# A two-block network: half-row heads, and half of an output product set between the turns of an attention

## Chip, cores and metric

One core of one Trainium2 chip runs the whole program in one launch. The metric is device time in microseconds (us), the median of several runs. In the profile PE is TensorE (PEld its weight loads), DVE is VectorE, ACT is ScalarE, POOL is GpSimd, SP is SyncE, whose queue issues most DMAs.

## What is computed

256 tokens of width 1024 pass two blocks in fp32. The first block has a mixer (spatial gating beside a neighbourhood attention with 8 heads of 64), a convolution mixer and two MLPs. The second block, cut to what the change touches:

```python
def hybrid_mixer(h, w_in, w_out, rel_bias):
    proj = h @ w_in                      # mq, mk, mv, dq, dk, dv, iq, ik, iw
    ...
    y_moba = moba_attention(mq, mk, mv, rel_bias[:8])      # 8 heads of 64
    y_dsa = dsa_attention(dq, dk, dv, iq, rms(ik), iw * 0.5, rel_bias[8:])
    return concatenate([y_moba, y_dsa]) @ w_out            # 1024 -> 1024

def dsa_attention(q, k, v, q_idx, k_idx, w_idx, tab):
    rel = relu(einsum('bqhd,bsd->bqhs', q_idx, k_idx))     # 4 index heads of 64
    score = einsum('bqh,bqhs->bqs', w_idx, rel)            # causal
    ...                                  # the 64 best keys of each query stay
    s = q @ k * scale + bias             # 8 heads of 64, on the keys that stay
    return softmax(s) @ v
```

After it come the gated sum `x + g1 * y`, a norm, and the peer feed-forward (queries by `w_q`, products with `subkeys`, then the large tables `uT` and others).

## The kernel before

**Products.** Weights arrive as fp32 tiles of 128 x 1024 through SP's queue (L146). ACT casts each to its high part (L176, fp32r), DVE or POOL makes the low part (L177). `mm` (L182 to L185) multiplies in three matmuls, hi by hi, hi by lo, lo by hi. The work is recorded for the Tile framework, which fixes at build time the order in which each engine takes its instructions. Each engine takes its own in that order.

**Attention.** A head has 64 rows of the 128 partitions; two heads lie in one tile `kT[:, f, :]`. The queries are copied into `qz`, a tile of 8 heads by 128 rows that was zeroed by POOL (`memset`, L712 and L1047) and of which each head fills its own 64 rows (`scaled_queries`, L628 to L633, 8 ACT instructions). A head's scores (L776 in the first mixer, L1128 in the second) are matmuls over all 128 rows, the other 64 being zeros. The index heads do the same with `iq` (memset L1074, copies L1076, transposes L1089, products L1100). `probs` (L612 to L626) adds the bias and takes the row's extreme on DVE (L618), the exponential on ACT (L620), the reciprocal and the scaling on DVE (L623, L625). Then PE turns the rows (L1142), ACT copies them (L1143), and for each pair of heads PE multiplies with the values (L1148), 64 columns of the array for each of the two. DVE copies the result (L1151), ACT casts its high part (L198), DVE makes its low part (L199), both into `yT`. `pipelined` (L635) runs `scores` some heads ahead of `values` (3 in moba, 2 in dsa), and before each turn takes one step of the generator `aside`.

**The second mixer** (`mixer2`, L1053). The moba projections come first. In the turns of the moba attention stand the index heads and the projections of dsa. DVE then finds the kept keys in eight rounds (L1166, L1168) and writes `kept` (L1171). In the dsa attention POOL adds `kept` to a head's bias, one instruction for each head and row tile, 16 in all (L1132). The output product with `w_out_2` runs in four parts of 256 rows: parts 0 and 1 (moba's half of `yT`) are 48 matmuls of 128x512 (`rows_step`, recorded ahead of the dsa attention), parts 2 and 3 (dsa's half) another 48 in `rows_end` (L474). `add_gated` (L447) multiplies the sums with the gate (L454) and adds them to x (L455), tile by tile of 128 tokens. The norm's rows are turned by L398, and the products with `w_q` begin (L191 to L194). The DMA of `subkeys` (L1288) opens the peer stage; it writes into a buffer that `yT` held.

Of the kernel before, what the change touches and what calls it, by code (L numbers as in the profile page):

```python
# [15 lines left out]
OP = mybir.AluOpType  # L16
# [3 lines left out]
P = 128  # L20
D = 1024
KC = D // P
T = 256
EPS = 1e-6
NEG = -1e30
# [49 lines left out]
class Net:  # L75
# [552 lines left out]
    def scaled_queries(self, qz, pq):  # L628

        for f in range(4):  # L630
            for j in range(2):
                s = slice(64 * j, 64 * j + 64)
                self.nc.scalar.mul(qz[s, 2 * f + j, :], pq[f // 2][s, f % 2, :], 0.125)  # L633
# [75 lines left out]
    def mixer0_rest(self, h, hc, qs, pgs):  # L709
        nc, a = self.nc, self.a  # L710
        qz = self.big([P, 8, T])
        nc.gpsimd.memset(qz, 0.0)  # L712
        self.scaled_queries(qz, qs)
# [51 lines left out]
        bts, pTs = {}, {}  # L765

        def scores(hd):
            f, j = hd // 2, hd % 2
            if j == 0:
                bt = bts[f] = self.work([P, 5, T], "bias", 2)  # L770
                nc.gpsimd.memset(bt[:, 4, :], 0.0)
                nc.sync.dma_start(bt[:, 0:4, :], a["bias0"][f])
            parts = []
            for t in range(2):
                s = self.ps()
                nc.tensor.matmul(s, qz[:, hd, t * P : (t + 1) * P], kT[:, f, :], start=True, stop=True)  # L776
# [255 lines left out]
    def projections(self, b0, h, by_tile=False):  # L1032
# [12 lines left out]
        qz = self.big([P, 8, T])  # L1045
        with self.behind(self.last_pow):
            nc.gpsimd.memset(qz, 0.0)  # L1047
        for pq in self.feature_product(b0, h):
            yield
        self.scaled_queries(qz, pq)  # L1050
        yield kT, qz, v


    def mixer2(self, h, mods):
# [5 lines left out]
        def index_heads():  # L1060

            w = sum((self.weights(a["w_idx"][:, 4 * q : 4 * q + 4, :], [P, 4, 324]) for q in range(2)), [])
            iqT = self.m4([P, 4, T])
# [3 lines left out]
            for t in range(2):  # L1067
# [4 lines left out]
                iq = self.m2([P, 4, P])  # L1072
                with self.behind(self.last_pow):
                    nc.gpsimd.memset(iq, 0.0)  # L1074
                for i in range(4):
                    nc.vector.tensor_copy(iq[:, i, 64 * (i % 2) : 64 * (i % 2) + 64], pi[:, 64 * i : 64 * i + 64])  # L1076
# [9 lines left out]
            for t, (iq, ik) in enumerate(rows):  # L1086
                pt = self.ps([P, 4, P])
                for i in range(4):
# [6 lines left out]
            for t in range(2):  # L1095
                n = (t + 1) * P
                sc = self.work([P, n], f"score{t}", 1)
                for i in range(4):
                    pi = self.ps([P, n])
                    nc.tensor.matmul(pi, iqT[:, i, t * P : (t + 1) * P], ikT[:, :n], start=True, stop=True)  # L1100
# [14 lines left out]
        def attention(kqv, o, keep):  # L1115
            kT, qz, v = kqv
            bts, pTs = {}, {}

            def scores(hd):
                f, j = hd // 2, hd % 2  # L1120
                if j == 0:
                    bts[f] = self.work([P, 2, 3 * P], "bias", 3)
                    nc.sync.dma_start(bts[f], a["bias2"][o + f])
                parts = []
                s = self.ps([P, 3 * P])
                for t in range(2):
                    n, cs = (t + 1) * P, slice(t * P, (2 * t + 1) * P)
                    nc.tensor.matmul(s[:, cs], qz[:, hd, t * P : (t + 1) * P], kT[:, f, :n], start=True, stop=True)  # L1128
                    b = bts[f][:, j, cs]
# [392 lines left out]
```

## Time and profile before

| | us |
|---|---|
| median of 3 runs | 1743.08 |
| the runs | 1734.59, 1743.08, 1744.27 |
| the profiled execution's own time | 1740.32 |
| its span in the trace | 1738.5 |
| first mixer's attention | 122 to 175 |
| moba attention, index heads, dsa projections | 783 to 842 |
| first half of the output product | 842 to 852.7 |
| dsa attention | 852.7 to 881 |

The span runs from the first to the last instruction in the trace, and the execution's own time is some 2 us longer. The page gives busy time by engine and by line over the whole span; windows cut it into stretches; the timeline and the chain of waits give single instructions.

### The profile page before, as it was taken

The page shows a single profiled execution, that of the slowest core. Times are in us where ns is not written, and L with a number is a line of the kernel's source. Part 1 is how long each engine was busy: PE and PEld are TensorE (multiplying, and loading weights), DVE is VectorE, ACT ScalarE, POOL GpSimd, SP SyncE. Part 2 cuts the span into 40 slices and gives each one's busy share as a digit, 9 for nine tenths or more (in the row PEclk, how much of TensorE's full clock was granted, in tenths as well). Part 3 has the DMA queues.
Part 4 walks back from the last instruction along what each step waited for, and adds up shares of the span by engine and source line. Part 5 has one row for each costly group of instructions (what it writes and reads, how often), then busy time and mean ns, then how long its engine had stood idle before and what let it go on. Part 6 is the DMA issues. An engine that isn't in the chain of part 4 may idle for free.

```text
span 1738.5 us, 27382 instructions
## 1 busy us (share of the span) xinstructions
PE 1650.5 (95%) x10522; PEld 1462.9 (84%) x10522; DVE 1348.4 (78%) x1976; ACT 895.2 (51%) x1296; POOL 349.7 (20%) x201
## 2 busy tenths in 40 slices
PE   7997999999979999899989998999999999999998
PEld 4874799988857998687779998999999998888886
DVE  7879699986957999857678999888845556666665
ACT  7646576652126666646544445555554445444443
POOL 0113144430002554310328870000000000000001
PEclk9998999999979999999989999999999999999999
DMA  9765599956405999474155655877787667998871
GB/s 371 242 240 206 175 330 322 351 201 218 147 25 212 348 334 336 148 255 146 58 192 193 198 184 188 275 247 250 251 282 242 212 214 252 323 337 295 267 239 49
DMA packets 145142, 406.63 MB, mean 234 GB/s; under 512 B 12786, under 2 KB 45810, under 8 KB 142835
## 3 DMA queue, kind: packets, MB, share of 16 engines
q1 hardware_dynamic: 137280, 390.66, 65.7%
q10 hardware_dynamic: 7474, 14.16, 2.1%
q8 instruction: 82, 1.34, 0.3%
q14 instruction: 50, 0.40, 0.1%
q0 software_dynamic: 256, 0.07, 0.0%
HBM read 374.43 MB, written 30.41 MB: 233 GB/s over the span
## 4 chain that ended last, share of the span: by engine, by line
PE 76%; DVE 9%; issue 4%; ACT 3%; POOL 2%; DMA 1%; SPq 0%; POOLq 0%; DVEq 0%; ACTq 0%
PE ps L183 9%; PE ps L185 8%; PE ps L184 8%; PE acc L185 7%; PE acc L184 7%; PE acc L183 7%; PE pa L185 6%; PE pa L183 6%; PE pa L184 6%; PE acc L1273 3%; PE ps L581 2%; PE ps L870 1%; POOL lo L177 1%; DMA st<-w_mod 1%; DVE m L861 1%
## 5 line engine op out<-in xcount | busy, mean ns | idle before, releaser
L176 ACT CAST hi<-st 128x1024 fp32r<-128x1024 f32 x466 | 476.8, 1046 | 422.5 <-PE pa L184 169.2
L177 DVE TENSOR_TENSOR lo<-st,hi 128x1024 fp32r<-128x1024 f32 x418 | 515.2, 1258 | 160.4 <-ACT hi L176 146.8
L183 PE MATMUL pa<-k,hi 128*128 128x256 f32 x1024 | 291.8, 285 | 1.9 <-ACT act L1319 1.9
L185 PE MATMUL pa<-k,lo 128*128 128x256 f32 x1024 | 288.4, 282 | 2.6 <-POOL lo L177 2.6
L184 PE MATMUL pa<-k,hi 128*128 128x256 f32 x1024 | 288.1, 281 | 0.0
L183 PE MATMUL ps<-k,hi 128*128 128x256 f32 x816 | 229.0, 281 | 0.1
L184 PE MATMUL ps<-k,hi 128*128 128x256 f32 x816 | 228.8, 281 | 0.0
L185 PE MATMUL ps<-k,lo 128*128 128x256 f32 x816 | 228.8, 281 | 0.0
L185 PE MATMUL acc<-hi,m 128*128 128x512 f32 x512 | 199.5, 390 | 0.0
L184 PE MATMUL acc<-lo,m 128*128 128x512 f32 x512 | 199.5, 390 | 0.0
L183 PE MATMUL acc<-hi,m 128*128 128x512 f32 x512 | 199.2, 389 | 0.0
L185 PEld LDWEIGHTS pa<-k,lo 128*128 128x128 f32 x1024 | 195.5, 191 | 3.2 <-POOL lo L177 3.2
L183 PEld LDWEIGHTS pa<-k,hi 128*128 128x128 f32 x1024 | 194.2, 190 | 2.7 <-ACT act L1319 2.1
L184 PEld LDWEIGHTS pa<-k,hi 128*128 128x128 f32 x1024 | 195.4, 191 | 0.5
L304 POOL TENSOR_TENSOR k<-k,st 128x1024 f32<-128x1024 f32 x48 | 142.5, 2971 | 174.2 <-ACT st L303 173.0
L183 PEld LDWEIGHTS ps<-k,hi 128*128 128x128 f32 x816 | 153.4, 188 | 2.9 <-DVE sh L319 0.9
L185 PEld LDWEIGHTS ps<-k,lo 128*128 128x128 f32 x816 | 155.5, 191 | 0.3 <-DVE lo L177 0.3
L184 PEld LDWEIGHTS ps<-k,hi 128*128 128x128 f32 x816 | 153.7, 188 | 1.6 <-DVE k L284 0.3
L945 POOL TENSOR_TENSOR k<-act,m 128x512 f32<-128x512 f32 x3 | 3.9, 1311 | 682.5 <-DVE act L943 682.5
L306 DVE SCALAR_TENSOR_TENSOR k<-st,sil,k 128x1024 f32<-128x1024 f32 x48 | 136.9, 2855 | 0.5
L177 POOL TENSOR_TENSOR lo<-st,hi 128x1024 fp32r<-128x1024 f32 x48 | 122.8, 2584 | 42.0 <-ACT hi L176 42.0
L185 PEld LDWEIGHTS acc<-hi,m 128*128 128x128 f32 x512 | 96.2, 188 | 20.0 <-DVE m L199 0.3
(297 smaller groups left out, 2994.9 us busy)
## 6 DMA issues: line engine op xcount, KB each, us to landing
st<-w_ff SPq DMA_DIRECT2D x128, 512.0 KB, 6.2
st<-uT SPq DMA_DIRECT2D x128, 512.0 KB, 4.5
st<-v SPq DMA_DIRECT2D x128, 512.0 KB, 5.0
st<-w_mod SPq DMA_DIRECT2D x96, 512.0 KB, 6.2
st<-w_ada SPq DMA_DIRECT2D x48, 512.0 KB, 7.0
st<-w_in SPq DMA_DIRECT2D x44, 512.0 KB, 6.3
gates<-k SPq DMA_DIRECT2D x16, 1024.0 KB, 7.5
k<-gates SPq DMA_DIRECT2D x16, 1024.0 KB, 7.8
```

The lines of the kernel that those rows point to most:

```text
L176: nc.scalar.copy(h, raw)
L177: self.last_lo = (lo or nc.vector).tensor_tensor(l, raw, h.bitcast(F32), op=OP.subtract)
L183: mm(ps, l.hi, r.hi, start=first, stop=False)
L184: mm(ps, l.hi, r.lo, start=False, stop=False)
L185: mm(ps, l.lo, r.hi, start=False, stop=last)
L304: nc.gpsimd.tensor_tensor(t[:, s], t[:, s], st, op=OP.add)
L306: nc.vector.scalar_tensor_tensor(t[:, s], st, by, t[:, s], op0=OP.mult, op1=OP.add)
L581: mm(p[:, j, :], wt[k][:, j * P : (j + 1) * P], h[:, k, :], start=k == 0, stop=k == KC - 1)
L861: nc.vector.scalar_tensor_tensor(v, z[:, i : i + T], self.col("w_dw", c * 31 + i), v, op0=OP.mult, op1=OP.add)
L870: nc.tensor.matmul(yt[t][c % 2][:, c // 2 * P : c // 2 * P + P], z[:, t * P + i : t * P + i + P], dg[:, i, :], start=i == 0, stop=False)
L945: (nc.vector if t and h else nc.gpsimd).tensor_tensor(dst[:, s], y, fg[:, s], op=OP.mult)
L1273: nc.tensor.matmul(pg[:, i, :], y[:, q + i, :], z[:, q + i, :], start=True, stop=True)
```

## The change

Heads are multiplied on their own 64 rows: `qT` has the two heads of a pair in one tile as `kT` has, and the scores of a pair are issued together, a head on rows 0 to 63 and one on rows 64 to 127, each into a PSUM tile of its own. No query tile is zeroed. The index heads do likewise (two turned tiles in place of four for a row tile). In dsa `keep` is one tile of 384 columns, and DVE adds it to the bias of two heads at once, four instructions of 128x768, in place of the 16 on POOL. The first half of the output product becomes `first_half`, a generator handed to `pipelined` as `aside`: it yields once, and then gives six matmuls a turn. Its arithmetic is the same.

```diff
-    def scaled_queries(self, qz, pq):
-        for f in range(4):
-            for j in range(2):
-                s = slice(64 * j, 64 * j + 64)
-                self.nc.scalar.mul(qz[s, 2 * f + j, :], pq[f // 2][s, f % 2, :], 0.125)
+    def scaled_queries(self, qT, pq):
+        for i in range(2):
+            self.nc.scalar.mul(qT[:, 2 * i : 2 * i + 2, :], pq[i], 0.125)
...
         nc, a = self.nc, self.a
-        qz = self.big([P, 8, T])
-        nc.gpsimd.memset(qz, 0.0)
-        self.scaled_queries(qz, qs)
+        qT = self.big([P, 4, T])
+        self.scaled_queries(qT, qs)
         bsp = self.m2([P, 512])
...
-        bts, pTs = {}, {}
+        bts, pTs, pss = {}, {}, {}
...
+                for t in range(2):
+                    for i in range(2):
+                        s = pss[hd + i, t] = self.ps()
+                        b = slice(64 * i, 64 * i + 64)
+                        nc.tensor.matmul(s, qT[b, f, t * P : (t + 1) * P], kT[b, f, :], start=True, stop=True)
             parts = []
             for t in range(2):
-                s = self.ps()
-                nc.tensor.matmul(s, qz[:, hd, t * P : (t + 1) * P], kT[:, f, :], start=True, stop=True)
+                s = pss.pop((hd, t))
                 i = 2 * j + t
...
             nc.any.tensor_copy(kT[:, 2 * i : 2 * i + 2, :], pk[i])
-        qz = self.big([P, 8, T])
-        with self.behind(self.last_pow):
-            nc.gpsimd.memset(qz, 0.0)
         for pq in self.feature_product(b0, h):
             yield
-        self.scaled_queries(qz, pq)
-        yield kT, qz, v
+        qT = self.big([P, 4, T])
+        self.scaled_queries(qT, pq)
+        yield kT, qT, v
...
             w = sum((self.weights(a["w_idx"][:, 4 * q : 4 * q + 4, :], [P, 4, 324]) for q in range(2)), [])
-            iqT = self.m4([P, 4, T])
+            iqT = self.m4([P, 2, T])
             ikT = self.m1([P, T])
...
                 nc.vector.tensor_scalar(iw[:, t, :], pi[:, 320:324], 0.5, None, op0=OP.mult)
-                iq = self.m2([P, 4, P])
-                with self.behind(self.last_pow):
-                    nc.gpsimd.memset(iq, 0.0)
-                for i in range(4):
-                    nc.vector.tensor_copy(iq[:, i, 64 * (i % 2) : 64 * (i % 2) + 64], pi[:, 64 * i : 64 * i + 64])
+                iq = self.m1([P, 2, P])
+                nc.vector.tensor_copy(iq, pi[:, 0:256].rearrange("p (a b) -> p a b", a=2))
                 sq = self.m1([P, 64])
...
             for t, (iq, ik) in enumerate(rows):
-                pt = self.ps([P, 4, P])
-                for i in range(4):
+                pt = self.ps([P, 2, P])
+                for i in range(2):
                     nc.tensor.transpose(pt[:, i, :], iq[:, i, :], self.ident)
...
                     pi = self.ps([P, n])
-                    nc.tensor.matmul(pi, iqT[:, i, t * P : (t + 1) * P], ikT[:, :n], start=True, stop=True)
+                    b = slice(64 * (i % 2), 64 * (i % 2) + 64)
+                    nc.tensor.matmul(pi, iqT[b, i // 2, t * P : (t + 1) * P], ikT[b, :n], start=True, stop=True)
                     rl = self.m1([P, n])
...
         def attention(kqv, o, keep):
-            kT, qz, v = kqv
-            bts, pTs = {}, {}
+            kT, qT, v = kqv
+            bts, pTs, pss = {}, {}, {}
...
                     nc.sync.dma_start(bts[f], a["bias2"][o + f])
+                    if keep is not None:
+                        nc.vector.tensor_tensor(bts[f], bts[f], keep.unsqueeze(1).to_broadcast([P, 2, 3 * P]), op=OP.add)
+                    for i in range(2):
+                        pss[hd + i] = self.ps([P, 3 * P])
+                    for t in range(2):
+                        for i in range(2):
+                            b = slice(64 * i, 64 * i + 64)
+                            nc.tensor.matmul(pss[hd + i][:, t * P : (2 * t + 1) * P], qT[b, f, t * P : (t + 1) * P],
+                                             kT[b, f, : (t + 1) * P], start=True, stop=True)
                 parts = []
-                s = self.ps([P, 3 * P])
+                s = pss.pop(hd)
                 for t in range(2):
                     n, cs = (t + 1) * P, slice(t * P, (2 * t + 1) * P)
-                    nc.tensor.matmul(s[:, cs], qz[:, hd, t * P : (t + 1) * P], kT[:, f, :n], start=True, stop=True)
-                    b = bts[f][:, j, cs]
-                    if keep is not None:
-                        bb = self.m1([P, n])
-                        nc.gpsimd.tensor_tensor(bb, b, keep[t], op=OP.add)
-                        b = bb
-                    parts.append((s[:, cs], b, n, None))
+                    parts.append((s[:, cs], bts[f][:, j, cs], n, None))
                 return self.probs(parts)
...
-        keep = []
+        keep = self.work([P, 3 * P], "kept", 1)
         for t in range(2):
...
                 cur = nxt
-            kp = self.work([P, n], f"kept{t}", 1)
-            nc.vector.tensor_scalar(kp, cur, GONE, NEG, op0=OP.not_equal, op1=OP.mult)
-            keep.append(kp)
+            nc.vector.tensor_scalar(keep[:, t * P : (2 * t + 1) * P], cur, GONE, NEG, op0=OP.not_equal, op1=OP.mult)
         accs = self.accs()
-        for b in range(2):
-            self.rows_step(accs, [self.rows_part(yT, "w_out_2", b)], b == 0, False)
-        self.pipelined(8, *attention(dsa, 4, keep), ahead=2)
+        def first_half():
+            yield
+            for b in range(2):
+                lhs, wt, ks = self.rows_part(yT, "w_out_2", b)
+                for t in range(2):
+                    for i in range(2):
+                        for j, k in enumerate(ks):
+                            self.mm(accs[t][i], lhs[:, k, t * P : (t + 1) * P], wt[j][:, i * 512 : (i + 1) * 512], k == 0, False)
+                        yield
+        self.pipelined(8, *attention(dsa, 4, keep), ahead=2, aside=first_half())
         h2, fill = self.modulated(self.col("nf2"), mods["s2"], mods["sh2"])
```

Below are rows of the built programs, in the order in which an engine takes them. Numbers behind a name tell buffers apart.

PE at the end of the dsa query projection, before (`ps_8090` to `ps_8093` are the four sums of the output product, `ps_8168` and `ps_8188` the scores of heads 0 and 1); ahead of these rows stand the other 44 matmuls of the first half:

```order
L185 MATMUL ps_8093<-hi_8132,k_1374_7286 128x512
L183 MATMUL ps_8093<-hi_8138,k_1373_7285 128x512
L184 MATMUL ps_8093<-lo_8139,k_1373_7285 128x512
L185 MATMUL ps_8093<-hi_8138,k_1374_7286 128x512
L1128 MATMUL ps_8168<-m_1539_7885,b_1540_7888 128x128
L1128 MATMUL ps_8168<-m_1539_7885,b_1540_7888 128x256
L1128 MATMUL ps_8188<-m_1539_7885,b_1540_7888 128x128
```

And the same place after (`ps_8056` to `ps_8059` are now the four sums, `ps_8063` and `ps_8064` the scores of heads 0 and 1):

```order
L185 MATMUL ps_7863<-k_1301_6794,lo_7935 128x256
L1129 MATMUL ps_8063<-m_1539_7859,b_1554_7986 128x128
L1129 MATMUL ps_8064<-m_1539_7859,b_1554_7986 128x128
L1129 MATMUL ps_8063<-m_1539_7859,b_1554_7986 128x256
L1129 MATMUL ps_8064<-m_1539_7859,b_1554_7986 128x256
L183 MATMUL ps_8056<-hi_8084,k_1373_7271 128x512
```

The row shown last and eleven more of the product are followed on PE by the second pair's scores and the first head's turned rows:

```order
L185 MATMUL ps_8057<-hi_8090,k_1374_7272 128x512
L1129 MATMUL ps_8122<-m_1539_7859,b_1554_7986 128x128
L1129 MATMUL ps_8123<-m_1539_7859,b_1554_7986 128x128
L1129 MATMUL ps_8122<-m_1539_7859,b_1554_7986 128x256
L1129 MATMUL ps_8123<-m_1539_7859,b_1554_7986 128x256
L1143 MATMUL ps_8142<-ident_71,m_1596_8070 128x128
```

The 48 matmuls stood ahead of the first scores; now the scores of heads 0 and 1 follow the projection, and the 48 stand in groups between later scores, transposes and values.

DVE from the last round of the kept keys to the first L618 of dsa, before and then after:

```order
L1171 TENSOR_SCALAR kept_1588_8088<-m_1587_8086 128x256
L177 TENSOR_TENSOR lo_8103<-st_8100,hi_8102 128x1024
L177 TENSOR_TENSOR lo_8133<-st_8130,hi_8132 128x1024
L177 TENSOR_TENSOR lo_8139<-st_8136,hi_8138 128x1024
L177 TENSOR_TENSOR lo_8425<-st_8422,hi_8424 128x1024
L177 TENSOR_TENSOR lo_8431<-st_8428,hi_8430 128x1024
L177 TENSOR_TENSOR lo_8447<-st_8444,hi_8446 128x1024
L618 ISA m_1610_8176,sm_1611_8177<-ps_8168,m_1607_8170 128x128
L618 ISA sm_1611_8177 128x1
```

```order
L1171 TENSOR_SCALAR kept_7989<-m_1587_8053 128x256
L1123 TENSOR_TENSOR bias_8060<-bias_8060,kept_7989 128x768
L1123 TENSOR_TENSOR bias_8119<-bias_8119,kept_7989 128x768
L177 TENSOR_TENSOR lo_8091<-st_8088,hi_8090 128x1024
L1123 TENSOR_TENSOR bias_8187<-bias_8187,kept_7989 128x768
L177 TENSOR_TENSOR lo_8218<-st_8215,hi_8217 128x1024
L618 ISA m_1596_8070,sm_1597_8071<-ps_8063,bias_8060 128x128
L618 ISA sm_1597_8071 128x1
L618 ISA m_1598_8074,sm_1599_8075<-ps_8063,bias_8060 128x256
```

Six casts of weights stood between `kept` and the first L618; now three additions and two casts do. The fourth addition stands 19 rows further on.

PE at the values of the last pair of heads (L1148, now L1149), before and after, the second half's matmuls around them:

```order
L1148 MATMUL ps_8409<-m_1699_8397,m_1524_7758 64x256
L185 MATMUL ps_8091<-b_1714_8434,k_1374_7286 128x512
L1148 MATMUL ps_8409<-m_1701_8403,m_1524_7758 64x256
L1148 MATMUL ps_8409<-m_1699_8397,m_1524_7758 64x128
L1148 MATMUL ps_8409<-m_1701_8403,m_1524_7758 64x128
L183 MATMUL ps_8092<-b_1714_8434,k_1373_7285 128x512
L184 MATMUL ps_8092<-b_1715_8435,k_1373_7285 128x512
```

```order
L184 MATMUL ps_8056<-lo_8363,k_1373_7271 128x512
L1149 MATMUL ps_8347<-m_1682_8335,m_1524_7732 64x256
L1149 MATMUL ps_8347<-m_1684_8341,m_1524_7732 64x256
L1149 MATMUL ps_8347<-m_1682_8335,m_1524_7732 64x128
L1149 MATMUL ps_8347<-m_1684_8341,m_1524_7732 64x128
L185 MATMUL ps_8056<-hi_8362,k_1374_7272 128x512
L183 MATMUL ps_8056<-hi_8368,k_1373_7271 128x512
```

Before, 24 of the second half's 48 matmuls stand behind the last of these values; after, 46, the first L398 among the last of them.

## Rows read from the trace of the kernel before

**Rows 1.** Page, part 1: busy us, share of the span, instructions.

```profile
PE 1650.5 (95%) x10522; PEld 1462.9 (84%) x10522; DVE 1348.4 (78%) x1976; ACT 895.2 (51%) x1296; POOL 349.7 (20%) x201
```

**Rows 2.** Windows around the second mixer: length, PE, PEld, DVE, ACT, POOL busy; PEclk, DMA.

```profile
783.00:842.00 59.00, 56.70 (x389) 48.93 (x388) 48.86 (x157) 36.13 (x83) 6.63 (x7) 1.00 0.46 143
842.00:852.70 10.70, 10.70 (x48) 8.80 (x47) 3.60 (x3) 5.16 (x9) 4.18 (x6) 1.00 0.14 38
852.70:881.00 28.30, 25.24 (x119) 16.72 (x118) 18.39 (x68) 14.13 (x46) 4.89 (x8) 0.88 0.00 0
858.00:866.00 8.00, 6.86 (x26) 4.45 (x26) 4.94 (x20) 3.25 (x13) 1.76 (x4) 0.57 0.00 0
906.00:940.00 34.00, 34.00 (x293) 34.00 (x292) 28.76 (x92) 15.13 (x21) 25.57 (x11) 1.00 0.58 187
```

**Rows 3.** Timeline of PE, 793 to 804: start us, us, what.

```profile
795.37 1.99 PE L1100 MATMUL ps<-m,m 128*128 128x256 f32 x8 [0.62 <-ACT m L1093]
797.30 0.86 PE L1148 MATMUL ps<-m,m 128*64 128x256 f32 x6
798.09 0.92 PE L1128 MATMUL ps<-m,b 128*128 128x128 f32 x4
...
801.94 0.82 PE L1128 MATMUL ps<-m,b 128*128 128x128 f32 x4
802.60 0.49 PE L1142 MATMUL ps<-ident,m 128*128 128x128 f32 x3
```

**Rows 4.** Timeline of DVE, 836 to 856.

```profile
838.83 0.29 DVE L1171 TENSOR_SCALAR kept<-m 128x256 f32<-128x256 f32 x1
...
853.31 1.23 DVE L177 TENSOR_TENSOR lo<-st,hi 128x1024 fp32r<-128x1024 f32 x1 [3.13 <-ACT hi L176]
854.45 0.28 DVE L618 CUSTOM_DVE_ANT_0 m<-ps,m 128x128 f32<-128x128 f32 x1
```

**Rows 5.** Timeline of DVE and PE, 878 to 901.

```profile
880.53 0.43 DVE L199 TENSOR_TENSOR k<-m,k 128x256 fp32r<-128x256 f32 x1 [0.47 <-ACT k L198]
...
887.10 1.06 PE L398 MATMUL ps<-ident,st 128*128 128x128 f32 x8 [1.80 <-DVE st L381]
...
889.05 0.68 DVE L454 TENSOR_TENSOR m<-ps,grow 128x512 f32<-128x512 f32 x1
...
890.71 0.42 PE L192 MATMUL ps<-lo,k 128*128 128x256 f32 x1
...
893.69 0.41 PE L192 MATMUL ps<-lo,k 128*128 128x256 f32 x1
...
895.61 1.32 PE L398 MATMUL ps<-ident,st 128*128 128x128 f32 x8
...
899.25 0.28 PE L192 MATMUL ps<-lo,k 128*128 128x256 f32 x1
899.37 0.29 PE L191 MATMUL ps<-hi,k 128*128 128x256 f32 x1
```

**Rows 6.** Timeline of SP's queue, 840 to 900.

```profile
885.10 0.33 SPq L1288 DMA_DIRECT2D k<-subkeys  x1
885.48 2.10 SPq L146 DMA_DIRECT2D st<-w_q  x4
...
891.93 5.40 SPq L146 DMA_DIRECT2D st<-w_q  x2
```

**Rows 7.** Groups by line, 122 to 176: busy us, mean ns, idle before.

```profile
L304 POOL TENSOR_TENSOR mod<-mod,st 128x1024 f32<-128x1024 f32 x8 | 20.5, 2567 | 10.6 <-ACT st L303 10.3
L625 DVE TENSOR_SCALAR m<-m,z 128x512 f32<-128x512 f32 x16 | 18.1, 1163 | 0.1
L776 PE MATMUL ps<-b,b 128*128 128x512 f32 x32 | 17.7, 670 | 0.0
```

**Rows 8.** Windows in the first mixer's attention, columns as in rows 2.

```profile
130.00:135.00 5.00, 3.88 (x11) 1.93 (x10) 4.96 (x6) 1.77 (x4) 4.84 (x3) 0.66 0.36 105
135.00:140.00 5.00, 0.90 (x5) 0.27 (x3) 5.00 (x2) 0.00 (x0) 4.74 (x2) 0.83 0.25 63
```

## The prediction

> **What bounds the kernel now.** Read the page's busy shares first [rows 1]: TensorE works 95% of the span and VectorE 78%. TensorE's time is nearly the whole time, but an average says nothing about one stage. So read next the windows around the second mixer [rows 2]. The first stretch, moba attention with projections and index heads, has TensorE busy 56.70 of 59.00 us: less TensorE work there is time saved. The second, 842.00 to 852.70, is 48 matmuls and nothing else, 10.70 of 10.70, .223 each: the first half of the output product. VectorE has 3.60 us of work in it and ScalarE 5.16; they have no scores to work on. The third, 852.70 to 881.00, is the dsa attention, 28.30 us: TensorE shows 25.24 busy, but at a mean granted clock of 0.88, and in its worst stretch, 858 to 866, at 0.57, near the lower level of 1.2 GHz; VectorE is busy 18.39. Neither engine is full in it, for each turn passes from TensorE to VectorE, ScalarE and back. From 906 on TensorE is busy 34.00 of 34.00, so what the mixer gains arrives there whole.
>
> **Term 1, half-row heads in the moba stage.** The timeline of TensorE [rows 3] prices a head's scores: the four records of one (every such matmul is two) begin at 801.94 and the next work at 802.60, .66. Two heads one after the other are 1.32, side by side .66. What leaving and entering the half-array form costs is not in the trace for rows, but it is for columns: the six records of the values at 797.30 (four of 256 columns, two of 128, 1.07 us one after another at .107 per 128, .53 side by side) are followed by the next instruction at 798.09, .79 later. So pairs do run together, and the way in and out costs .26. A pair of heads then takes .66 + .26 = .92 and saves .40: 1.6 for the four pairs of moba. The index heads are 4 scores on 128 keys and 4 on 256; the second four take 1.99 less a tail of .28, 1.71 [rows 3], the first four half of it, 2.56 together, 1.28 + 2 x .26 = 1.80 after: .76. Four of eight transposes go, .11 each (eight in 1.06 less a tail of .2 to .3 [rows 5]): .4. Sum 2.8, of which some falls into the 2.3 us that TensorE is idle: I take **-2.5**, bounds 0 (all of it idle time, or no pair runs together) and -3.5 (no cost of switching).
> The Trainium skill's page "TensorEngine Tiling (Array Packing)", Key Properties, says that changing the tiling mode drains TensorE, which speaks against short pairs between full matmuls. The trace agrees that the switch costs something, .26 for two. Priced as the tail of a record beyond its step at each switch (.28 shown for a step of .12 [rows 5], so .16, twice .32), an estimate, the sum 2.8 would be 2.4.
>
> **Term 2, dsa begins before the rows product.** Before, the first L618 is at 854.45 and waits for nothing but the scores that stand behind the 48 matmuls [rows 4]. The order shows the scores of heads 0 and 1 straight behind the query projection, which ends by 842. In their place VectorE's own queue now decides: behind `kept` (838.83 + .29 = 839.12) stand three of the new L1123 additions and two L177 casts, ahead of the first L618. An addition of 768 elements is not in the trace; 512 take .68 [rows 5] and 1024 take 1.23 [rows 4], so .96 lies between them (bounds .68 and 1.23). 839.12 + 3 x .96 + 2 x 1.23 = 844.46, against 854.45: **-10.0** (bounds -10.9 and -9.2), and the 2.5 of term 1 come on top, since kept, scores and queries all move with it. The 16 POOL additions L1132 go; nothing on this path waits for them but L618, and VectorE's additions take their place there.
>
> **Term 3, how long the attention lasts.** Before: 854.45 to the end of the last L199, 880.53 + .43 = 880.96 [rows 5], 26.5 us. VectorE's work in that time: 18.39 less the cast at 853.31 (1.2) is 17.2 with three L177 in it; the order now puts seven there, and one addition: 17.2 + 4 x 1.22 + .96 = 23.0. TensorE's, at full clock: four pairs of heads x .92, 24 transposes x .11, four sets of values x .79 and 48 matmuls x .223: 20.2. Both engines have work while the other turns, so TensorE need not stand idle as it does where the clock falls. The length lies between VectorE's 23.0 and the old 26.5 plus some waits of transposes behind six-matmul blocks of 1.34 us, say 28.5. I take 24.5, nearer to the work than to the old length, since VectorE would be over 90% busy: **-2.0** (bounds -3.5 and +2).
>
> **Term 4, the tail.** The other half of the rows product used to start inside the attention; by the order 24 of its 48 matmuls stood behind the last values. Now 46 do, 10.3 us. The chain that follows, before: L398 of the first row tile at 887.10, its w_q products at half clock from 890.71 to 893.69, .213 a step against .12 later, L398 of the second tile at 895.61, 14.65 after the last L199 [rows 5]. After: the first tile's sums come later by some 1.5, and its L398 stands inside the remaining rows, which end some 10.8 after the last L199 against 4.3; but then TensorE goes from rows to w_q products without the gap that lay between the L398 (887.10 + 1.06) and the products of w_q, so the 16 steps of .213 may run at .12 (-1.5). The second tile's additions, last at 889.05, 8.1 after, move behind the rows' end. I take **+0.5** at the second tile's L398, bounds -2 (clock kept, additions not moved) and +3 (both lost).
>
> **Term 5, the first mixer.** 16 scores as 32 records, 17.7 us shown, .85 each as two steps of .427 (512 columns at .107 per 128): in pairs 6.8 less [rows 7]. But there VectorE and POOL hold the time: in 130 to 140 VectorE is busy 4.96 and 5.00 of 5, TensorE 3.88 and 0.90 [rows 8], with POOL's L304 at 2.57 us beside L625 at 1.16 [rows 7]. I take **-1.0**, bounds -6.8 (all on the path) and +2 (four scores ahead of each pair delay the transposes behind them). Memsets of POOL and the scaled queries (8 ScalarE instructions into 2) lie under TensorE-bound stretches: 0.
>
> **Sum.** -2.5 - 10.0 - 2.0 + 0.5 - 1.0 = -15.0. The profiled execution took 1740.32, so 1725.3. It lies 2.8 under the median of the three runs shown, 1743.08, which spread over 9.7; the forecast is for a run like the profiled one.
>
> **The rivals.**
> A. *The second half eats it.* TensorE takes its queue in order: blocks of six matmuls stand ahead of transposes whose data is ready, so the attention keeps its 26.5 us, and 22 matmuls more than before stand behind the last values, 22 x .223 = 4.9, all of it on the chain. -2.5 - 10.0 + 4.9 - 1.0 = -8.6: 1731.7. For it: the order. Against it: the second tile's additions stand 8.1 after the last L199 already, so most of the 4.9 has room.
> B. *The pairs do not run together*, so the change doesn't do what it says: TensorE takes the halves one after another, with the cost of switching. Term 1 becomes +1, the attention 1.6 + 1 longer, term 5 0: -15 + 3.5 + 2.6 + 1 = 1732.5. Against it: the values' .79 for 1.07 [rows 3].
> C. *Late loads.* SP's transfer of the subkeys (885.10) waits for TensorE's last read of the mixer's output, and the loads of w_q and uT queue behind it, the last two issued from 891.93 to 897.33 [rows 6]. That point moves from 4.1 to some 10.8 after the last L199. If half or all of these 6.7 us come out at the peer's start, 3.4 to 6.7 are given back: about 1730. Against it: loads and products of the peer alternate, and TensorE is full from 906, well behind the last issue.
> D. *Slower: TensorE falls to its lower clock.* The granted clock is 0.57 in 858 to 866, where the turns leave TensorE waiting, and 1.00 in moba [rows 2], which has pairs over columns in it. Where the change leaves TensorE in short pairs with waits between, as in 858 to 866, work at 1.2 GHz costs as much again. The sign turns where more than 15 us of full-clock work falls to it; a third of moba's 56.7 gives +3.9, 1744; all of it +41.7, 1782. Against it: TensorE has a rows product to fill every turn.
> The skill's "TensorE: Matmul & The Clock Gate", Why this matters, says that a single matmul with few rows takes as long as a full one, and only tiles running together gain; that is the condition between my forecast and B, and no run here shows it for rows.
>
> **How the numbers follow.** Forecast .63, A .15, B .07, C .10, D .05. Range: the ends of terms 3 to 5 do not fall together; the favourable ends of terms 1 to 3 with half of those of 4 and 5 give some -22, and A with a poor term 3 and 5 gives -4. So 1717 to 1737. A measurement of this kernel can tell about 0.5%, 8.7 us. Faster by more: .95 of the forecast, half of A, .4 of B and .65 of C: .60 + .07 + .03 + .07 = .77. Slower by more: most of D and a little of the rest, .05. Within: .18.
>
> **What would show it.** Right: the first L618 near 842 instead of 854.45, no stretch of 48 matmuls alone, the granted clock at 1.00 from there to the second tile's L398, last L199 near 866.5, L398 of the second tile near 881, the peer's full TensorE from about 892; L1128's successor with two records at one start. Wrong: scores' records strictly one after another (B); the attention longer than 27 us with TensorE waiting on nothing but its own order (A); a stretch near 890 in which TensorE waits for w_q or uT (C); a clock of 0.5 before 840 (D). The forecast fails upwards if VectorE's casts hold the softmax of the last heads, and downwards if the first mixer was waiting for TensorE after all.

## Result and profile after

The changed kernel took 1720.6 us, median of 4 runs (1715.87 to 1725.03), against 1740.26 before, also of 4: ratio 0.9894, 95% interval 0.9863 to 0.9925, 13 to 24 us faster. Timed again (below) the ratio was 0.9915 (0.9886 to 0.9944). The forecast was 1725.3. The profiled execution after took 1721.3, its span 1719.2.

The page's first part after, to compare with [rows 1]:

```profile
PE 1630.8 (95%) x10518; PEld 1446.2 (84%) x10518; DVE 1343.1 (78%) x1973; ACT 888.6 (52%) x1279; POOL 329.5 (19%) x180
```

Windows of the second mixer after (columns as in [rows 2]): from the index heads' first transpose to the end of `kept`, the dsa attention, and three stretches of the tail.

```profile
781.05:830.54 49.49, 46.49 (x318) 37.35 (x316) 42.25 (x136) 28.00 (x69) 3.04 (x3) 0.97 0.51 160
834.00:861.00 27.00, 26.99 (x149) 17.98 (x148) 22.71 (x74) 18.86 (x52) 0.00 (x0) 1.00 0.06 15
861.00:872.00 11.00, 10.26 (x50) 8.03 (x49) 6.66 (x14) 4.84 (x13) 0.55 (x1) 1.00 0.01 1
872.00:885.00 13.00, 8.64 (x66) 7.66 (x65) 10.64 (x31) 9.30 (x18) 5.18 (x4) 0.98 0.98 369
885.00:920.00 35.00, 35.00 (x292) 35.00 (x292) 29.16 (x93) 15.25 (x21) 25.95 (x12) 0.96 0.67 238
```

And before, the stretch that answers to the first line:

```profile
788.36:839.12 50.76, 48.46 (x328) 40.87 (x327) 43.03 (x138) 29.85 (x71) 3.37 (x4) 1.00 0.50 156
```

The stretch of 48 matmuls alone is gone. In the attention TensorE is busy 26.99 of 27.00 us at a granted clock of 1.00, where it was 25.24 of 28.30 at 0.88 [rows 2]. VectorE's timeline after answers to [rows 4, 5]:

```profile
830.25 0.28 DVE L1171 TENSOR_SCALAR kept<-m 128x256 f32<-128x256 f32 x1
830.57 1.83 DVE L1123 TENSOR_TENSOR bias<-bias,kept 128x768 f32<-128x768 f32 x2
...
835.46 0.28 DVE L618 CUSTOM_DVE_ANT_0 m<-ps,bias 128x128 f32<-128x128 f32 x1
...
860.68 0.42 DVE L199 TENSOR_TENSOR k<-m,k 128x256 fp32r<-128x256 f32 x1
...
871.48 0.69 DVE L454 TENSOR_TENSOR m<-ps,grow 128x512 f32<-128x512 f32 x1 [0.94 <-PE ps L185]
```

From the end of `kept` to the first L618 of the dsa attention it is now 4.92 us (15.33 before), from there to the last L199's end 25.64 (26.50).

One trace before and one after can't carry the comparison, as the runs below show. Four traces of the kernel before and three of the changed one give this, in us, in the order in which they were taken:

| stretch | before | after |
|---|---|---|
| first mixer, first L618 to the start of the last copy of values | 51.57, 51.69, 49.75, 51.66 | 49.93, 48.45, 50.58 |
| TensorE waiting for L381 at the second mixer's norm | 0.75, 1.80, 2.00, 1.63 | 0, 0, 0 |
| index transposes to end of `kept` | 50.76 in all four | 49.49, 49.57, 49.62 |
| end of `kept` to first L618 of dsa | 15.33, 15.78, 15.35, 15.78 | 4.92, 4.97, 4.92 |
| first L618 to end of last L199 | 26.50, 23.95, 25.28, 25.10 | 25.64, 25.94, 25.62 |
| from there to the second query transposes | 24.11, 21.48, 23.20, 21.70 | 23.17, 23.18, 23.16 |
| the last three together | 65.94, 61.21, 63.83, 62.58 | 53.73, 54.09, 53.70 |
| from there to the end of the last DMA issue | 830.3, 831.3, 829.8, 829.2 | 831.8, 829.1, 830.2 |

The three stretches around the dsa attention carry 9.6 us (63.4 against 53.8 in the mean), the rest comes from smaller places, some of it from the granted clock, and nothing is given back later.

### The profile page after: what moved, and what is told of

It reads as the page before. It is cut to its first block, busy times and chain, and to the rows that moved or that the text cites. A ratio compares the mean times of both kernels' runs of the same rounds, so it can differ in the third digit from the quotient of the medians.

```text
span 1719.2 us, 27324 instructions
## 1 busy us (share of the span) xinstructions
PE 1630.8 (95%) x10518; PEld 1446.2 (84%) x10518; DVE 1343.1 (78%) x1973; ACT 888.6 (52%) x1279; POOL 329.5 (19%) x180
## 4 chain that ended last, share of the span: by engine, by line
PE 80%; DVE 9%; issue 4%; ACT 3%; POOL 2%; DMA 2%; SPq 0%; POOLq 0%; DVEq 0%; ACTq 0%
PE ps L183 10%; PE ps L185 10%; PE ps L184 10%; PE acc L185 7%; PE acc L184 7%; PE acc L183 7%; PE pa L185 6%; PE pa L183 6%; PE pa L184 6%; PE acc L1282 3%; PE ps L581 2%; PE ps L872 1%; POOL lo L177 1%; DVE m L863 1%; DVE lo L177 1%
## 5 line engine op out<-in xcount | busy, mean ns | idle before, releaser
L306 DVE SCALAR_TENSOR_TENSOR k<-st,sil,k 128x1024 f32<-128x1024 f32 x48 | 132.6, 2765 | 0.5
```

The lines of the kernel that those rows point to most:

```text
L306: nc.vector.scalar_tensor_tensor(t[:, s], st, by, t[:, s], op0=OP.mult, op1=OP.add)
```

## Experiments

**The two kernels again.** No edit.

> The kernel before, unchanged, for a second trace. In the two traces at hand 3.4 us of the 19 gained lie at 503 to 510 us, in eight L503 matmuls that the change does not touch: 0.85 us each at a granted clock of 0.50 before, 0.43 after. Theory: which clock they get differs from execution to execution, so this trace may show either, and 0.43 here takes 3.4 us off the gain that belongs to the change. Rival: the slower clock there belongs to the kernel before; then they take 0.85 again. Everything in the second mixer, by the theory, is as in the first trace: first L618 of dsa 15.6 us (15 to 16) after kept, last L199 26 to 27 us after that L618.

> The changed kernel, unchanged, for a second trace. Theory: the eight L503 matmuls may take 0.43 or 0.85 us each here; second mixer as in the first trace: kept to first L618 4.9 to 5.2 us, attention 25.2 to 26 us, TensorE busy over 99% in it at a granted clock of 1.00. Rival (the clock at 503 us belongs to the kernel): 0.43 each again.

The kernel before took 1734.81, the changed one 1714.69. The eight L503 matmuls ran at some 0.45 us a step in both. Over the fourteen traces of this study both speeds occur on either side: slow in the first and the fourth trace of the kernel before and in four with the change, fast in the other eight. So 3 us of the first pair's difference were the clock's and not the change's. And the dsa attention before took 23.95, not the 26 to 27 that the theory had from the trace that the forecast read. A window of this second trace:

```profile
858.00:866.00 8.00, 8.00 (x43) 5.11 (x44) 5.46 (x24) 4.45 (x18) 2.27 (x4) 1.00 0.00 0
```

[rows 2] has 6.86 busy at 0.57 for the same microseconds.

**The move taken back, and the move alone.** The first variant puts back the loop of `rows_step` ahead of the attention, the second puts `first_half` into the kernel before.

```diff
-        def first_half(): ...
-        self.pipelined(8, *attention(dsa, 4, keep), ahead=2, aside=first_half())
+        for b in range(2):
+            self.rows_step(accs, [self.rows_part(yT, "w_out_2", b)], b == 0, False)
+        self.pipelined(8, *attention(dsa, 4, keep), ahead=2)
```

> The changed kernel with the first half of the output product back ahead of the dsa attention (pairs, unpadded queries and the additions on VectorE stay). Theory: the move carries 10 to 11 us of the gain, the rest some 5 (moba and index heads 2 to 3, first mixer 1.7, dsa scores 1.6), so 5 us faster than before, ratio 0.995 to 0.999, and some 11 to 13 slower than the changed kernel; the first L618 of dsa stands behind 48 matmuls again. Rival: the pairs and the additions carry it, since VectorE's order is what frees the attention: over 12 us faster than before, ratio under 0.993.

> The kernel before with only the first half of the output product moved between the turns (zero-padded queries over 128 rows, POOL's 16 additions, all memsets stay). Theory: 10 to 13 us faster than before, ratio 0.9925 to 0.9945, first L618 of dsa 3 to 5 us after kept. Rival: POOL's additions, one for each head and tile and up to 1.7 us each beside VectorE, now set the pace of the attention, which gets longer than 28 us: 5 us faster or less, ratio over 0.997.

Without the move: ratio 0.9926 (0.9898 to 0.9954), where the theory had 0.995 to 0.999; the number is the rival's. The move alone: 0.9925 (0.9899 to 0.9951), as its theory had it. Together that would be 26 us, more than the whole change. As times these two can't be told from each other, and hardly from the whole change, since each of the three intervals is 9 to 11 us wide. The traces tell them apart. Without the move the first L618 comes 16.64 us after `kept`, and the stretch from `kept` to the second query takes 59.2; with the move alone it takes 4.02 and 53.65, as in the changed kernel. So with the move the pairs and VectorE's additions add nothing in this stretch; without it they are worth 2 us or more (59.2 against 61.2 to 65.9). With the move alone the attention is longer, 28.77, as the rival had it, but TensorE is busy 28.25 of it, and POOL's additions beside paired heads (below) take 26.24: so TensorE sets most of that length, not POOL. The tail behind it is shorter (20.87 against 23.17). The variant without the move gains the rest in the other rows of the table.

**The first mixer as before.** Zeroed query tile and scores over 128 rows there; the second mixer as changed.

```diff
+        qz = self.big([P, 8, T])
+        nc.gpsimd.memset(qz, 0.0)
+        self.padded_queries(qz, qs)
...
+                nc.tensor.matmul(s, qz[:, hd, t * P : (t + 1) * P], kT[:, f, :], start=True, stop=True)
```

> The changed kernel with the first mixer's heads as before (zeroed query tile, scores over 128 rows, one at a time). Theory: VectorE and POOL hold the time there, so 1 to 2 us slower than the changed kernel, ratio to before about 0.990; the last L800 copy near 174.7 instead of 172.8. Rival: TensorE was waited for in the first mixer, so 4 to 7 us slower than the changed kernel, ratio about 0.993.

Ratio 0.991 (0.9871 to 0.995), last copy at 175.19: near the theory's numbers, though 0.991 is also what the changed kernel has when it is timed again (0.9915). Its attention, 49.88 from first L618 to last copy, is no longer than the changed kernel's. The loss lies before it, at 58 to 65 us, and led to the memset below.

**POOL's additions instead of VectorE's.**

```diff
-                    if keep is not None:
-                        nc.vector.tensor_tensor(bts[f], bts[f], keep.unsqueeze(1).to_broadcast([P, 2, 3 * P]), op=OP.add)
...
+                        nc.gpsimd.tensor_tensor(bb, b, keep[:, cs], op=OP.add)
```

> The changed kernel with the 16 additions of kept to the bias on POOL, as before, in place of the 4 on VectorE. Theory: after the change TensorE is busy 26.99 of 27.00 us in the attention, so who adds matters only at its start: three additions (2.8 us) leave VectorE's queue ahead of the first L618, but the scores end at 834.97 against 835.46, so at most 0.5 us is gained there, and VectorE's casts and scalings beside POOL get slower; within 1.5 us of the changed kernel. Rival: VectorE bounds the attention (22.7 of 27 busy, three additions on the path), so POOL's additions make it 2 to 4 us faster.

Ratio 0.9923 (0.9896 to 0.995). `kept` to L618 4.61, attention 26.24, to the second query 23.26: 54.1 together, as without the edit. Where the additions stand makes no difference that these runs can show.

**Heads of a pair one after the other in the queue.**

```diff
-                    for t in range(2):
-                        for i in range(2):
+                    for i in range(2):
+                        for t in range(2):
```

> The changed kernel with the scores of a pair in the second mixer issued head by head (128 and 256 columns of the first head, then of the second), so that only two of the four matmuls can run beside another. Nothing else changes. Theory: halves run side by side only when their neighbours in the queue are on other rows; a pair of heads takes some 1.1 to 1.3 us in place of 0.86, 8 pairs cost 2 to 3.5 us more. Rival: the gain of half rows is in less work, not in running together: no change, under 0.5 us.

This fell. Ratio 0.9923 (0.9899 to 0.9947), `kept` to second query 54.3. TensorE's timeline of this variant, where a pair's eight records stand:

```profile
839.67 0.28 PE L185 MATMUL ps<-k,lo 128*128 128x256 f32 x1
839.88 0.93 PE L1129 MATMUL ps<-m,b 64*128 64x128 f32 x8
840.74 0.50 PE L183 MATMUL ps<-hi,k 128*128 128x512 f32 x1
```

0.86 from start to next start, to the hundredth what the changed kernel has (below). By the records' own starts the second head begins 13 ns after the first, although the first head's other matmul stands ahead of it, and all four records of 128 columns begin before the four of 256.

**Timed again, and two more traces of the kernel before.** No edit.

> The changed kernel timed in five rounds on one chip with two more traces of the kernel before. From the traces so far the stretch from the end of kept to the second query transposes (L1364) takes 53.7 to 54.3 us in five kernels with the move, at a granted clock of 1.00, and 65.9 and 61.2 in two traces of the kernel before, which differ by the clock alone. Theory: the stretch is 53.5 to 54.5 again and the time 13 to 20 us under the kernel before, ratio 0.9885 to 0.9925. Rival: the first measurement was a lucky one, and the change is worth what the stage sums without any clock say, 7 for this stretch and 3 for the rest, ratio 0.994.

> The kernel before, for a third trace. Theory: the attention of dsa leaves TensorE waiting, so in some executions its clock falls there and in some not: 61 to 66 us from the end of kept to the second query transposes, with attention 24 us where the clock stays at 1.00 and 26 to 27 where it falls to 0.5 to 0.6 around the first turns. Rival: the fall in the first trace was a single event; 61 again.

> The kernel before, for a fourth trace, with the same theory and rival as for the third: 61 to 66 us from the end of kept to the second query transposes, the clock falling in some of the executions; or 61 in every one but the first.

1726.18 in 6 runs against 1738.71 in 10, ratio 0.9915, and the stretch 53.70: both as the theory had them. (The two medians alone lie 12.5 apart.) The kernel before gave 63.83 and 62.58, inside the theory's range and not the 61 of the rival; its attention, 25.28 and 25.10 at a mean clock of 0.93, lies between the theory's two cases. In the fourth trace the clock fell at the same place in the turns as in the first, for fewer microseconds:

```profile
866.00:870.00 4.00, 3.31 (x11) 2.07 (x12) 3.20 (x14) 1.97 (x7) 1.18 (x2) 0.57 0.00 0
```

**The memset.** One dead memset is put where the zeroed query tile had its own.

```diff
+        idle = self.big([P, 8, T])
+        nc.gpsimd.memset(idle, 0.0)
         qT = self.big([P, 4, T])
```

> The changed kernel with one dead POOL memset of 128x2048 put back where the first mixer's zeroed query tile had its own; nothing reads it. In five of six traces of kernels with that memset, VectorE's L381 at 58 us takes 3.7 to 4.0 us (0.48 alone), two memsets of POOL long, and TensorE is idle 1.3 to 1.6 us behind it; in the first trace of the kernel before, and in six traces without it, 2.0 to 2.3 us and no idle time. Theory: the memset, not the half rows, is what the first 70 us gained: L381 3.7 to 4.0 us again, TensorE idle 1.3 to 1.6 us between 60 and 65 us, the first scores (L775) 1.5 us later, 1 to 2 us slower than the changed kernel. Rival: the gain there comes from the shorter scaling of the queries; L381 2.0 to 2.3 us, no idle time.

Ratio 0.9931 (0.9906 to 0.9957), median 1722.43 in 12 runs: the 1 to 2 us can't be read from that. The timeline of POOL, VectorE and TensorE of this variant can:

```profile
58.92 1.81 POOL L710 MEMSET b<- 128x2048 f32 x1
60.67 1.81 POOL L294 MEMSET mod<- 128x2048 f32 x1
...
59.01 4.00 DVE L381 TENSOR_SCALAR m<-st,sm 128x512 f32<-128x512 f32 x1 [0.66 <-POOL sm L375]
...
63.07 1.09 PE L398 MATMUL ps<-ident,m 128*128 128x128 f32 x8 [0.64 <-DVE m L381]
64.79 0.38 PE L183 MATMUL ps<-k,hi 128*128 128x256 f32 x1 [0.63 <-DVE b L655]
```

The changed kernel:

```profile
57.96 1.81 POOL L294 MEMSET mod<- 128x2048 f32 x1
...
58.05 2.25 DVE L381 TENSOR_SCALAR m<-st,sm 128x512 f32<-128x512 f32 x1 [0.67 <-POOL sm L375]
...
60.43 1.91 PE L398 MATMUL ps<-ident,m 128*128 128x128 f32 x16
```

A memset that nobody reads holds VectorE's L381 (0.48 us a few microseconds earlier) for the length of both memsets, and TensorE waits twice, 1.27 us in all. Six of the seven traces with this memset show it, three of the four of the kernel before among them, and none of the seven without. The first trace of the kernel before, which the forecast read, was the seventh. There L381 took 2.00, no wait behind it, and POOL's second memset took 2.09 instead of 1.81. From L381 to the first L618 of the first mixer it is 66.6 to 67.7 us in the six and 64.7 to 65.9 in the eight others, so the loss stays to there.

**Without the first half.** The 48 matmuls are left out (moba's half of the output product isn't computed); casts and loads stay, and the second half begins the sums.

```diff
-                        for j, k in enumerate(ks):
-                            self.mm(accs[t][i], lhs[:, k, t * P : (t + 1) * P], wt[j][:, i * 512 : (i + 1) * 512], k == 0, False)
                         yield
...
-        self.rows_end(accs, parts, False, mods["g1"], fill)
+        self.rows_end(accs, parts, True, mods["g1"], fill)
```

> The changed kernel with the 48 matmuls of the first half of the output product left out (moba's half of y is not multiplied; its weights are loaded and cast as before). This measures what the 10.7 us of matmuls cost between the turns. Theory: TensorE is busy 26.99 of 27.00 us in the attention and VectorE 22.7 of 27, so the attention ends when VectorE's work does: 22 to 23.5 us in place of 25.6, and 50 to 52 us from the end of kept to the second query transposes in place of 53.7 to 54.3; 7 to 9 us of the 10.7 are hidden. Rival: TensorE alone is the bound, and the attention shortens to 16 to 19 us.

This fell too. 10.7 us of TensorE work less, and the kernel is no faster: ratio 0.9943 (0.992 to 0.9965), attention 24.66 instead of 25.64, `kept` to second query 60.75 instead of 53.7. Windows of the attention in this variant:

```profile
834.00:840.00 6.00, 2.79 (x8) 1.25 (x8) 5.94 (x27) 5.44 (x16) 0.00 (x0) 0.66 0.20 66
840.00:846.00 6.00, 6.00 (x22) 3.48 (x22) 4.11 (x17) 3.88 (x11) 0.00 (x0) 0.50 0.00 0
846.00:852.00 6.00, 5.57 (x23) 2.70 (x24) 3.59 (x17) 3.46 (x14) 0.00 (x0) 0.70 0.01 4
```

TensorE waits for the softmax in the first turns, its granted clock falls to 1.2 GHz, and the turns after run at that. The rest has other reasons: four casts instead of two stand ahead of the first L618 in VectorE's queue (7.21 after `kept` instead of 4.92), and in the tail, 28.88 instead of 23.17, the first L398 now stands ahead of the second tile's matmuls in TensorE's queue and waits 3.66 us there. So the variant doesn't price the 48 matmuls cleanly. The attention without them took 24.66 here and 22.48 in the variant without the move, both at a lower mean clock (0.72 and 0.85), and 25.6 to 25.9 with them in the changed kernel: it has room for most of them. What they cost at one and the same clock no run shows. In all eight traces that have them there the clock is 1.00 throughout the attention.

## Why the prediction was right

**Term 1 (-2.5): right in kind, half in size (-1.2).** A pair's scores take 0.86 us by TensorE's timeline after (0.92 foretold), and its records start together:

```profile
834.11 0.93 PE L1129 MATMUL ps<-m,b 64*128 64x128 f32 x8
834.97 0.50 PE L183 MATMUL ps<-hi,k 128*128 128x512 f32 x1
```

TensorE's work in the stretch fell by 1.97, but its length only by 1.2 (50.76 to 49.5): TensorE now waits 3.0 there instead of 2.3, and the granted clock is 0.97 in the mean instead of 1.00. At the index heads one wait, 0.82 before, is 1.99 long, and behind it the granted clock is 0.57 in the mean of 4 us, near the lower level of 1.2 GHz. After, then before (windows with the columns of [rows 2]):

```profile
784.94 0.30 PE L1089 MATMUL ps<-ident,m 128*128 128x128 f32 x1 [1.99 <-DVE m L1080]
781.00:785.00 4.00, 1.90 (x16) 1.11 (x15) 3.54 (x10) 3.92 (x10) 0.55 (x1) 1.00 0.48 129
785.00:789.00 4.00, 4.00 (x24) 2.78 (x25) 3.11 (x20) 3.36 (x15) 0.00 (x0) 0.57 0.79 228
```

```profile
788.00:792.00 4.00, 3.18 (x23) 2.64 (x23) 3.36 (x17) 3.85 (x12) 0.55 (x1) 1.00 0.33 71
792.00:796.00 4.00, 3.38 (x23) 2.61 (x22) 3.99 (x19) 4.00 (x16) 0.00 (x0) 1.00 0.89 278
```

The 4.00 us of work at 0.57 would take 1.7 less at 1.00 (an estimate), enough for the 1.3 that the term lacks. The long wait and the fall stand in all nine traces with pairs in this stage and in none of the five without. The step that failed is that the forecast put moba's clock at 1.00 and its waits at those of before.

The way in and out of the half rows costs 0.22 for a pair (0.86 less 0.64). The Trainium skill's "TensorEngine Tiling (Array Packing)", Key Properties, says that a change of the tiling mode drains TensorE; the trace agrees that the change costs something. The forecast's .26 for columns is a misreading of [rows 3]. The six records are four of 128 columns and two of 256, by the view of this line (ns of the shortest, the median and the longest; first and last start; forms):

```profile
L1148 PE MATMUL ps<-m,m x6: 273/298/430, 797.3 to 797.9; 128*64 128x128 f32 x4, 128*64 128x256 f32 x2
```

That is .86 one after another, not 1.07, and the half with both of the 256 needs .64 of the .79, so .15 is left for the way in and out.

**Term 2 (-10.0): -10.4**, 4.92 after `kept` instead of 15.33, and -10.6 in the mean; the addition of 768 took 0.96 as interpolated. With term 1's shift and those before it the first L618 came at 835.46, not near 842. One reading was wrong: before, the first L618 didn't wait for its scores alone. It stands in VectorE's queue behind the cast at 853.31, which had waited 3.13 for ScalarE's cast [rows 4], and that one, by the profile, 3.49 for one of the 48 matmuls; head 0's scores began earlier:

```profile
852.23 1.99 ACT L176 CAST hi<-st 128x1024 fp32r<-128x1024 f32 x2 [3.49 <-PE ps L185]
852.72 2.13 PE L1128 MATMUL ps<-m,b 128*128 128x128 f32 x12
```

So the 48 matmuls held up the attention in two ways, ahead of the scores and by way of the casts, and the casts came later. The wait of 3.13 stands in all five traces without the move and in none with it.

**Term 3 (-2.0): -0.9 in this pair, and +0.5 in the mean** (25.2 before, 25.7 after). The step that failed is TensorE's 20.2 us of work. It is 27.0. Of the 6.8 more, the values are 2.1: a set is eight records, of which the forecast priced the six that start together, and in three of four sets a matmul of the product stands between the first two and the six, so the way in and out is paid twice,

```profile
841.03 0.65 PE L1149 MATMUL ps<-m,m 128*64 128x256 f32 x2
841.61 0.51 PE L183 MATMUL ps<-hi,k 128*128 128x512 f32 x1
842.04 0.86 PE L1149 MATMUL ps<-m,m 128*64 128x256 f32 x6
842.84 0.51 PE L184 MATMUL ps<-lo,k 128*128 128x512 f32 x1
```

(0.58 + 0.80 here and 1.18 for the set that isn't split, instead of 0.79). Eleven matmuls of the second half, which run before the last L199, are 2.5. The last 2.4 are the product's matmuls next to another form, 0.32 to 0.48 each instead of 0.22, like the two in these rows; the scores are 0.2 less. VectorE's 23.0 was 21.3 (from the first L618 to the last L199; TensorE is busy 25.63 of these 25.64), so after the change TensorE is the bound, not VectorE. The old 26.5, taken from one execution, was the longest of four.

**Term 4 (+0.5): -0.15 in this pair**, the second tile's L398 14.50 after the last L199 (14.66), **and +0.5 in the mean** (13.97 before). The sums came late as foretold (last L454 10.4 after, 8.1 before), and the clock stayed up, so w_q's products ran at 0.12 a step and paid for it:

```profile
868.08 1.06 PE L398 MATMUL ps<-ident,st 128*128 128x128 f32 x8 [0.56 <-DVE st L381]
...
871.84 0.28 PE L192 MATMUL ps<-lo,k 128*128 128x256 f32 x1
871.96 0.28 PE L191 MATMUL ps<-hi,k 128*128 128x256 f32 x1
...
875.59 1.15 PE L398 MATMUL ps<-ident,st 128*128 128x128 f32 x8 [0.81 <-DVE st L381]
...
884.27 0.64 PE L1364 MATMUL ps<-ident,m 128*128 128x128 f32 x2 [1.89 <-ACT m L1361]
```

**Term 5 (-1.0): about right in number for the attention** (51.2 to 49.7 in the mean; over all fourteen traces 50.7 with zeroed tiles and 49.6 with pairs, ranges that overlap; the one run that takes the pairs out in the first mixer alone has 49.9, so that the pairs are worth it isn't shown), **wrong for the memsets.** "Memsets of POOL and the scaled queries lie under TensorE-bound stretches: 0" is the step that failed, and by the most: it is worth 1.3 us at 58 us in three of four executions, and 0.75 to 2.00 at the second mixer's norm in all four. The second was there to be read in the trace of before, in the timeline of POOL, VectorE and TensorE:

```profile
741.20 3.56 POOL L1047 MEMSET b<- 128x2048 f32 x2
744.70 1.00 POOL L1074 MEMSET m<- 128x512 f32 x2
...
741.31 4.67 DVE L381 TENSOR_SCALAR st<-st,sm 128x512 f32<-128x512 f32 x1 [0.93 <-POOL sm L976]
...
746.03 1.10 PE L398 MATMUL ps<-ident,st 128*128 128x128 f32 x8 [0.75 <-DVE st L381]
```

After, L381 takes 0.48 there and TensorE doesn't wait. No run takes these memsets out alone; the wait stands in all five traces that have them and in none of the nine without. L381 starts 0.11 us after the first memset and takes 4.2 us longer, the length of all four that POOL has in a row. The Trainium skill's "SBUF — State Buffer", Who interferes with whom, says that an instruction of VectorE in a two-port mode, which `tensor_scalar` can enter, and one of GpSimd lock a pair of ports against each other, and that the second to come is blocked for the whole of the first; the trace agrees with the blocking, here through four instructions and at 58 us through two. In which mode L381 runs no trace shows. The forecast didn't weigh that page.

**The rivals.** A: the order does put more behind the last values, but the second tile's chain absorbed most of it (term 4). B, whose sum is 1732.4: the halves run together. C: the loads start 10.1 after the last L199 instead of 4.1, and the second query's transposes wait 1.89 us for ScalarE, whose queue holds two casts of weights ahead of the copy; but from L398 to there it is 8.7, within the 7.8 to 9.5 before, so little was given back. D: the clock is 1.00 throughout the attention, where it was the kernel before whose clock fell; but at moba's index heads it does fall (term 1), the sign of D at a small price.

By the table's means the parts give 9.6 + 1.2 + 1.5 (norm) + 1.0 (first memset, three of four) + 1.5 (first mixer's attention) = 14.8, the 15 of the forecast from partly other sources; the two measurements lie at 18 and 15 by their ratios. The spans of the table's seven traces differ by 17.0 in the mean. Of the 2.2 that are left, 0.6 stand at L503 and some 1.1 between the norm and the index heads, where the clock falls in all four traces before and in two of the three after. That the sum came out is in part luck: terms 1 and 3 promised 4.5 where the means show 0.7 (1.2 gained, 0.5 lost), and the memsets, put at nothing, made up 2.5.

## What to carry over

Independent matmuls moved into the gaps of a stage that waits from engine to engine were worth here nearly the time that they took alone: the stretch fell from 63.4 in the mean to 53.7 with the move alone, for 10.7 us of matmuls. The gaps were then full, TensorE busy 25.6 of 25.6, so count with the queue's order what each switch between forms costs. Before charging an off-path memset at nothing, look at what VectorE does in the same microseconds: an instruction ten times its usual length beside POOL is the sign. And take two or three traces of the kernel before where the clock falls in some stretch, for this stage differed by nearly 5 us (61.2 to 65.9) between four executions of one kernel, in the order of its mean clock there (0.97 to 0.87).

## What was not expected of the hardware

Matmuls on the two row halves didn't keep the queue's order among each other: with the first head's two matmuls ahead of the second head's, the halves still start 13 ns apart, and the pair takes 0.86 us either way. And taking 10.7 us of work from TensorE made the stage slower, 60.75 instead of 53.7, with a lower clock and another order of casts and of the tail; how much each of the two costs no run separates.
